# A two-layer hybrid trunk on one core: RWKV's loop in four array quarters, GLA sums before scores, value weights loaded earlier

## The chip, the core and the metric

One NeuronCore of a Trainium2 chip. The metric is the device time of one execution in microseconds, the median of three runs. A kernel here is a program of five engines with a queue each: TensorE (PE) for matrix products, VectorE (DVE), ScalarE (ACT), GpSimd (POOL) and SyncE (SP), which issues most loads.

## What is computed

A trunk of two layers on 512 tokens of width 1024, with a memory of 256 rows. Everything is float32. Layer 0 mixes with gated linear attention (GLA, 4 heads, keys of 64, values of 128) beside RWKV-7 (8 heads of 64), layer 1 with an RG-LRU beside an mLSTM. After each mixer come a cross attention to the memory and a gated FFN. Cut to what the change touches:

```python
# GLA, per chunk of 64: scores within the chunk, state across chunks
scores = where(causal, q_dec @ k_inv.T, 0);  o = scores @ v + q_dec @ S
S = S * state_decay + k_end.T @ v
# RWKV-7, per chunk
z = z_state @ S + z_local          # (I - A_ab)^-1 applied: a triangular solve
y = r_dec @ S + A_rb @ z + y_local
S = S * state_decay + z.T @ b_end + v.T @ k_end
# cross attention, both layers: k, v = split(rms_norm(mem) @ xattn_wkv[layer])
```

## The kernel before

Activations are held transposed, 128 channels by 512 tokens a tile. A dense product with a weight block is done as three passes in a reduced float32 form: the block (512 KB) is loaded by SP into a ring of three `raw` buffers, ScalarE rounds it to `wh`, VectorE takes the rest as `wl` (rings of two each), and TensorE adds wh·xh, wh·xl and wl·xh (`wload`, L238; `dense`, L258). All of these instructions stand under the helper lines L192 (VectorE tensor-tensor), L204 (ScalarE) and L207 (products), so groups are told apart by the names of their tiles. PSUM has eight banks: three called `mm` for dense products and five called `ax` for all the rest.

The order on each engine comes from a planner that goes by program order as priority and puts later instructions in where earlier ones would wait. `issue_after` keeps a few in a chosen place.

GLA (`gla`, L602) projects q, k, v, then per head pair `p` computes masked scores into `SC` (L700 to L708), then the chunk sums and the state scan `S` (L709 to L724), then the outputs.

RWKV (`rwkv`, L777) prepares its operands per head pair (L808 to L875): `stk` and `SV` for the two heads `e` of a pair, `BB` with the masked products. Then the triangular solve (L877 to L915): 32x32 blocks are inverted in 31 steps of two VectorE instructions (`tm`, `tu`), the result is transposed back (L896, L898), and two groups of 32x32 products join the two blocks of each 64. Then the loop over 8 chunks (L931 to L960): w = stk·SV, copied to `ws`; y's first half; z = BB·ws, copied to `SV`; the state sum `uu`; y's second half from BB and z, copied to `yt`. A 64x64 product of head `e` uses rows `R[e]` and columns `R[e]` of the array, that is, one of two diagonal quarters.

The memory's keys and values for both layers (`memory_k`, L528; `memory_v`, L548) come last in the program order of this part (`after`, L1306), and the planner lays them into the solve and the loop. Layer 0's keys are done from raw float32 weights without conversion, eight blocks in the `raw` ring; its values need `wh` and `wl`, 512 columns by two k-blocks a piece, two halves of four pieces.

## Time and profile before

| | us |
|---|---|
| median of 3 runs | 1544.91 (1544.68 to 1545.15) |
| profiled execution | 1545.02 |
| its span | 1543.2 |
| TensorE busy | 1518.2 (98%) |
| TensorE weight loads busy | 1235.4 (80%) |
| VectorE busy | 912.6 (59%) |
| ScalarE busy | 688.7 (45%) |

A product in float32 is run by TensorE as two passes, so 8 products are 16 records. "PE" is the products, "PEld" the weight loads that overlap them; since products are pipelined, the length of a group is better read from its weight loads. A merged row of the timeline gives the start, the busy time of the group, and in brackets how long the engine was idle before it and what ended that.

### The profile page before, as it was taken

To read this page: it belongs to the slowest core of one execution; us is meant where nothing else is said; L and a number is where in the kernel's file an instruction comes from. 1 tells how busy PE (TensorE), PEld (TensorE's weight loads), DVE (VectorE), ACT (ScalarE), POOL (GpSimd) and SP (SyncE) were. 2 spreads that over 40 slices of the span, in tenths; PEclk is the share of its full clock that TensorE was granted. 3 is DMA by queue.
4 is the path that set the end of the run, shared out by engine and by line. 5 is a ranking of instruction groups with operands and counts; after the bars stand their busy time and mean duration, and the time that the engine had idled before them with its cause. 6 is when DMAs were issued, how large, how long until landed. Compare 5 with 4: busy or idle time off the path is not lost.

```text
span 1543.2 us, 20154 instructions
## 1 busy us (share of the span) xinstructions
PE 1518.2 (98%) x8069; PEld 1235.4 (80%) x8069; DVE 912.6 (59%) x1341; ACT 688.7 (45%) x1105; POOL 25.5 (2%) x64
## 2 busy tenths in 40 slices
PE   9999998999999999999999999999999999999998
PEld 7977776778888888888888777788888888888887
DVE  7548679564645756555533377677457656565333
ACT  6466553364434633333322367556336333333322
POOL 2000000110000000000000000000000000000000
PEclk9999998999999999999999999999999999999999
DMA  5222235236421433333333421225114333333332
GB/s 179 69 75 84 67 103 158 90 116 227 137 62 48 124 96 96 96 96 100 89 100 97 121 63 56 75 75 175 45 55 123 96 96 96 96 96 91 101 99 79
DMA packets 49599, 152.19 MB, mean 99 GB/s; under 512 B 5489, under 2 KB 7953, under 8 KB 49505
## 3 DMA queue, kind: packets, MB, share of 16 engines
q1 hardware_dynamic: 45120, 142.28, 30.7%
q10 hardware_dynamic: 3248, 5.11, 0.9%
q0 software_dynamic: 1136, 3.51, 0.7%
q8 instruction: 63, 1.03, 0.3%
q14 instruction: 32, 0.25, 0.0%
HBM read 144.59 MB, written 6.29 MB: 98 GB/s over the span
## 4 chain that ended last, share of the span: by engine, by line
PE 87%; DVE 7%; ACT 3%; issue 2%; DMA 1%; POOL 0%; SPq 0%; DVEq 0%; ACTq 0%
PE mm L207 76%; PE ax L207 10%; DVE wl L192 1%; ACT wh L204 1%; PE ax L462 1%; DMA raw<-in_w_kv 0%; DVE tm L192 0%; ACT e L204 0%; DVE tu L192 0%; ACT xs L204 0%; DVE au L887 0%; DVE xs L192 0%; DMA x<-in_xT 0%; ACT a L204 0%; DVE stk L201 0%
## 5 line engine op out<-in xcount | busy, mean ns | idle before, releaser
L207 PE MATMUL mm<-xs,wh 128*128 128x512 f32 (+1 forms) x3627 | 1105.6, 386 | 0.0
L207 PEld LDWEIGHTS mm<-xs,wh 128*128 128x128 f32 x3627 | 672.0, 188 | 144.6 <-issue 7.2
L207 PE MATMUL mm<-xs,wl 128*128 128x512 f32 (+1 forms) x1814 | 701.2, 387 | 0.0
L204 ACT ACTIVATE wh<-raw 128x1024 fp32r<-128x1024 f32 (+2 forms) x274 | 265.0, 967 | 536.2 <-PE mm L207 429.1
L192 DVE TENSOR_TENSOR wl<-raw,wh 128x1024 fp32r<-128x1024 f32 (+2 forms) x273 | 302.6, 1109 | 216.7 <-ACT wh L204 215.7
L207 PEld LDWEIGHTS mm<-xs,wl 128*128 128x128 f32 x1814 | 340.8, 188 | 71.0 <-issue 2.4
L192 DVE TENSOR_TENSOR h<-h,mm 128x512 f32<-128x512 f32 (+1 forms) x73 | 49.5, 678 | 80.2 <-PE mm L207 80.2
L192 DVE TENSOR_TENSOR upad<-mm,rstd 128x512 f32<-128x512 f32 (+1 forms) x52 | 35.9, 690 | 95.5 <-PE mm L207 95.3
L192 DVE TENSOR_TENSOR g<-mm,rstd 128x512 f32<-128x512 f32 (+1 forms) x44 | 30.4, 692 | 76.0 <-PE mm L207 75.9
L201 DVE SCALAR_TENSOR_TENSOR c<-upad,vec,c 128x512 f32<-128x512 f32 (+1 forms) x88 | 65.9, 749 | 3.3 <-ACT c L204 1.8
L207 PE MATMUL mm<-wh,xs 128*128 128x256 f32 (+1 forms) x256 | 67.6, 354 | 0.0
L204 ACT ACTIVATE c<-c 128x512 f32<-128x512 f32 (+1 forms) x44 | 27.8, 632 | 87.1 <-DVE c L201 87.1
L207 PEld LDWEIGHTS mm<-wh,xs 128*128 128x128 f32 x256 | 45.1, 196 | 6.4 <-ACT kt L204 0.8
L207 PE MATMUL mm<-wl,xs 128*128 128x256 f32 (+1 forms) x128 | 45.1, 353 | 2.9 <-DVE wl L192 2.9
L204 ACT ACTIVATE xs<-g 128x512 fp32r<-128x512 f32 (+1 forms) x44 | 27.9, 633 | 26.6 <-DVE g L192 26.6
L192 DVE TENSOR_TENSOR xs<-ax,xs 128x512 fp32r<-128x512 f32 (+1 forms) x36 | 24.0, 686 | 20.8 <-ACT xs L204 20.8
L204 ACT ACTIVATE c<-upad,vec 128x512 f32<-128x512 f32 (+1 forms) x44 | 35.3, 803 | 1.5 <-DVE upad L192 1.5
L192 DVE TENSOR_TENSOR g<-c,g 128x512 f32<-128x512 f32 (+1 forms) x44 | 30.4, 692 | 5.8 <-ACT c L204 1.4
L192 DVE TENSOR_TENSOR nacc<-nacc,nsq 128x512 f32<-128x512 f32 x45 | 32.8, 729 | 0.7 <-ACT nsq L204 0.6
L201 DVE SCALAR_TENSOR_TENSOR xs<-h,vec,xs 128x512 fp32r<-128x512 f32 x40 | 29.9, 749 | 3.5 <-ACT xs L204 3.4
L204 ACT ACTIVATE xs<-h,vec 128x512 fp32r<-128x512 f32 x40 | 28.8, 719 | 6.6 <-DVE h L192 6.6
L192 DVE TENSOR_TENSOR xs<-g,xs 128x512 fp32r<-128x512 f32 (+1 forms) x44 | 30.1, 685 | 2.5 <-ACT xs L204 2.5
(354 smaller groups left out, 1194.0 us busy)
## 6 DMA issues: line engine op xcount, KB each, us to landing
raw<-in_w_up SPq DMA_DIRECT2D x86, 512.0 KB, 3.5
raw<-in_w_dn SPq DMA_DIRECT2D x32, 512.0 KB, 3.5
raw<-in_w_kk SPq DMA_DIRECT2D x16, 512.0 KB, 3.6
raw<-in_w_kv SPq DMA_DIRECT2D x16, 512.0 KB, 4.1
raw<-in_w_q SPq DMA_DIRECT2D x16, 512.0 KB, 3.7
raw<-in_w_o SPq DMA_DIRECT2D x32, 256.0 KB, 2.7
raw<-in_w_cd SPq DMA_DIRECT2D x16, 512.0 KB, 3.6
raw<-in_w_rw SPq DMA_DIRECT2D x14, 512.0 KB, 3.8
```

The source lines that it names most:

```text
L192: (eng or self.nc.vector).tensor_tensor(out=out, in0=a, in1=b, op=op)
L201: return self.nc.vector.scalar_tensor_tensor(out=out, in0=a, scalar=s, in1=b, op0=op0, op1=op1)
L204: return self.nc.scalar.activation(out=out, in_=a, func=f, **kw)
L207: self.last_mm = self.nc.tensor.matmul(out, lhsT=l, rhs=r, start=start, stop=stop)
L462: nc.tensor.transpose(pT[m][:, t * P:(t + 1) * P], es[t][:, m * P:(m + 1) * P], K.ident)
```

## The change

Four edits. `memory_k` of layer 0 calls a function ahead of its fifth block that issues the load and the conversion of the first two value pieces; `memory_v` uses them. In GLA, each head pair's chunk sums and state scan come ahead of its scores and masks. At the end of the solve one transposition of all 128 partitions into a new tile `TT` replaces four of 32 partitions into `BB`; four copies (two on each of VectorE and ScalarE) bring it to `BB`, placed behind the first product group, and the second group reads `TT`. In the loop, head pairs 2 and 3 write the other column half, so that z and y's second half use all four quarters; z and y have two banks each (z's second lies in w's bank), and their evictions are split accordingly; y becomes one tile.

```diff
--- before.py
+++ after.py
@@ -525,11 +525,13 @@
     return X
 
 
-def memory_k(K, l, X, stage):
+def memory_k(K, l, X, stage, midway=None):
 
     nc = K.nc
     kd = K.dram.tile([P, 2048], F32, name=f"kd{l}")
     for j in range(0, KD, 2):
+        if midway and j == 4:
+            midway()
         st = stage.tile([P, T], F32, name="kvs")
         for i in range(2):
             if type(X[0]) is tuple:
@@ -545,14 +547,18 @@
     return kd
 
 
-def memory_v(K, l, X, stage):
+def v_weights(K, l, half, c):
+    return K.wload(K.I[f"w_kv{l}"][:, half, 2 * c:2 * c + 2], 2, 512)
+
+
+def memory_v(K, l, X, stage, early=()):
 
     nc = K.nc
     vd = K.dram.tile([P, 2048], F32, name=f"vd{l}")
     for half in range(2):
         ps = [K.mm.tile([P, T], F32, name="mm") for _ in range(2)]
         for c in range(4):
-            wh, wl = K.wload(K.I[f"w_kv{l}"][:, half, 2 * c:2 * c + 2], 2, 512)
+            wh, wl = early[c] if half == 0 and c < len(early) else v_weights(K, l, half, c)
             for m in range(2):
                 ms = slice(m * P, (m + 1) * P)
                 for k in range(2):
@@ -697,15 +703,6 @@
                         K.mmul(o, xh[:, ts], wl[:, k], False, c == 1 and k == 3 and t % 2 == 1)
             for t in range(4):
                 K.act(v[:, t, half * 256:(half + 1) * 256], ps[t // 2][:, t % 2], AF.Copy, scale=rt[:, t:t + 1])
-        for p in range(2):
-            ps = [K.ax.tile([P, 4, P], F32, name="ax") for _ in range(2)]
-            for t in range(4):
-                ts = slice(t * P, (t + 1) * P)
-                for e in range(2):
-                    r = slice(64 * e, 64 * e + 64)
-                    K.mmul(ps[e][:, t], ki[p][r, ts], qd[p][r, ts])
-            for e in range(2):
-                nc.vector.copy_predicated(out=SC[2 * p + e], mask=gm.to_broadcast([P, 4, P]), data=ps[e])
         S = gp.tile([P, 2, 7, P], F32, name="S")
         for p in range(2):
             us = [K.ax.tile([P, 4, P], F32, name="ax") for _ in range(2)]
@@ -722,6 +719,15 @@
                     K.act(S[:, p, 0], u, AF.Copy)
                 else:
                     K.stt(S[:, p, c], S[:, p, c - 1], sd[p][:, c, 63:64], u, ALU.mult, ALU.add)
+            ps = [K.ax.tile([P, 4, P], F32, name="ax") for _ in range(2)]
+            for t in range(4):
+                ts = slice(t * P, (t + 1) * P)
+                for e in range(2):
+                    r = slice(64 * e, 64 * e + 64)
+                    K.mmul(ps[e][:, t], ki[p][r, ts], qd[p][r, ts])
+            for e in range(2):
+                nc.vector.copy_predicated(out=SC[2 * p + e], mask=gm.to_broadcast([P, 4, P]), data=ps[e])
+
         def outputs(p):
 
             os = [K.ax.tile([P, T], F32, name="ax") for _ in range(2)]
@@ -894,8 +900,8 @@
                 K.add(Tt[:, s + 1:, 0:s + 1], Tt[:, s + 1:, 0:s + 1], tv)
             TN = A
             nc.vector.transpose(out=TN.rearrange("p u c -> p c u"), in_=Tt.rearrange("p l c -> p c l"))
-            for q in (1, 3, 0, 2):
-                nc.vector.transpose(out=units[Q[q], :, H[q % 2]].rearrange("p u l -> p l u"), in_=Tt[Q[q]])
+            TT = sp.tile([P, 32, 32], F32, name="tt")
+            nc.vector.transpose(out=TT.rearrange("p u l -> p l u"), in_=Tt)
             VV = sp.tile([P, 32, 32], F32, name="vv")
             for b in range(2):
                 ps = K.ax.tile([P, 16, 32], F32, name="ax")
@@ -905,12 +911,17 @@
                         K.mmul(ps[Q[2 * e + 1], u], units[Q[2 * e], 16 * b + u, 32:64], TN[Q[2 * e], 16 * b + u])
                 for e in range(2):
                     K.act(VV[Q[2 * e + 1], us], ps[Q[2 * e + 1]], AF.Copy)
+            for q in range(4):
+                if q % 2:
+                    K.act(units[Q[q], :, H[1]], TT[Q[q]], AF.Copy)
+                else:
+                    nc.vector.tensor_copy(out=units[Q[q], :, H[0]], in_=TT[Q[q]])
             for b in range(2):
                 ps = K.ax.tile([P, 16, 32], F32, name="ax")
                 us = slice(16 * b, 16 * b + 16)
                 for u in range(16):
                     for e in range(2):
-                        K.mmul(ps[Q[2 * e], u], VV[Q[2 * e + 1], 16 * b + u], units[Q[2 * e + 1], 16 * b + u, 32:64])
+                        K.mmul(ps[Q[2 * e], u], VV[Q[2 * e + 1], 16 * b + u], TT[Q[2 * e + 1], 16 * b + u])
                 for e in range(2):
                     K.act(units[Q[2 * e], us, 32:64], ps[Q[2 * e]], AF.Copy)
         with ExitStack() as es:
@@ -919,7 +930,9 @@
             nc.vector.memset(S, 0.0)
             for e in range(2):
                 nc.vector.memset(SV[e][R[e], 0], 0.0)
-            yt = [st.tile([P, T], F32, name=f"y{p}", bufs=1) for p in range(4)]
+            yt = st.tile([P, 4, T], F32, name="y", bufs=1)
+
+            O = [(p, e, R[e if p < 2 else 1 - e]) for i in range(2) for p in (i, 2 + i) for e in range(2)]
 
             def group(products):
 
@@ -929,21 +942,21 @@
                         f()
 
             for c in range(8):
-                w = K.ax.tile([P, 4, 64], F32, name="ax")
-                yp = K.ax.tile([P, 4, 64], F32, name="ax")
+                w = K.ax.tile([P, 8, 64], F32, name="ax")
+                yp = [K.ax.tile([P, 2, 64], F32, name="ax") for _ in range(2)]
                 group([lambda e=e, p=p: K.mmul(w[R[e], p], stk[e][:, p, c, 0:64], SV[e][:, c, p])
                        for p in range(4) for e in (1, 0)])
                 ws = st.tile([P, 4, 64], F32, name="ws")
-                nc.vector.tensor_copy(out=ws, in_=w)
-                for p in range(4):
-                    for e in range(2):
-                        K.mmul(yp[R[e], p], SV[e][:, c, p], stk[e][:, p, c, 64:128], p == 0, False)
-                z = K.ax.tile([P, 4, 64], F32, name="ax")
-                for p in range(4):
-                    for e in range(2):
-                        K.mmul(z[R[e], p], BB[R[e], p, c, 0:64], ws[R[e], p])
-                nc.vector.tensor_copy(out=SV[0][R[0], c], in_=z[R[0]])
-                K.act(SV[1][R[1], c], z[R[1]], AF.Copy)
+                nc.vector.tensor_copy(out=ws, in_=w[:, 0:4])
+                for p, e, o in O:
+                    K.mmul(yp[p // 2][o, p % 2], SV[e][:, c, p], stk[e][:, p, c, 64:128], p % 2 == 0, False)
+
+                z = (K.ax.tile([P, 2, 64], F32, name="ax"), w[:, 4:6])
+                for p, e, o in O:
+                    K.mmul(z[p // 2][o, p % 2], BB[R[e], p, c, 0:64], ws[R[e], p])
+                for s, o in ((slice(0, 2), 0), (slice(2, 4), 1)):
+                    nc.vector.tensor_copy(out=SV[0][R[0], c, s], in_=z[o][R[o]])
+                    K.act(SV[1][R[1], c, s], z[o][R[1 - o]], AF.Copy)
                 if c < 7:
                     uu = K.ax.tile([P, 4, 64], F32, name="ax")
                     group([lambda e=e, p=p: K.mmul(uu[R[e], p], BKT[:, p, c, R[e]], SV[e][:, c, p])
@@ -954,14 +967,16 @@
                     for e in range(2):
                         K.mul(SV[e][R[e], c + 1], t[R[e]], sb[R[e]].to_broadcast([64, 4, 64]))
                     K.mul(S, t, sb.to_broadcast([P, 4, 64]), nc.gpsimd)
-                group([lambda e=e, p=p: K.mmul(yp[R[e], p], SV[e][R[e], c, p], BB[R[e], p, c, 64:128], False, p == 3)
-                       for p in range(4) for e in (1, 0)])
-                for p in range(4):
-                    K.act(yt[p][:, c * 64:c * 64 + 64], yp[:, p], AF.Copy)
+                group([lambda e=e, p=p, o=o: K.mmul(yp[p // 2][o, p % 2], SV[e][R[e], c, p], BB[R[e], p, c, 64:128],
+                                                           False, p % 2 == 1) for p, e, o in O])
+                cs = slice(c * 64, c * 64 + 64)
+                K.act(yt[:, 0:2, cs], yp[0], AF.Copy)
+                for e in range(2):
+                    K.act(yt[R[e], 2:4, cs], yp[1][R[1 - e]], AF.Copy)
             g2 = K.qr.tile([P, T], F32, name="xs")
             nc.gpsimd.dma_start(out=g2, in_=K.I["w_g2"])
             for p in range(4):
-                y = yt[p]
+                y = yt[:, p]
                 ps = K.ax.tile([P, T], F32, name="ax")
                 K.mmul(ps, K.bo64m, y)
                 K.tt(y, y, ps, ALU.subtract)
@@ -1304,11 +1319,13 @@
                 M[:] = next(M[0])
 
         def after(stage):
-            kv.append([memory_k(K, 0, [t[:, s] for t in M for s in (slice(0, 256), slice(256, 512))], stage)])
+            early = []
+            kv.append([memory_k(K, 0, [t[:, s] for t in M for s in (slice(0, 256), slice(256, 512))], stage,
+                                lambda: early.extend(v_weights(K, 0, 0, c) for c in range(2)))])
             for h in range(4):
                 Y[h] = K.split(K.pr[0], Y[h])
             ms = memory_split(K, M)
-            kv[0].append(memory_v(K, 0, ms, stage))
+            kv[0].append(memory_v(K, 0, ms, stage, early))
             kv.append([memory_k(K, 1, ms, stage), memory_v(K, 1, ms, stage)])
 
         rwkv(K, X, Y, during, after)
```

## Rows read from the trace of the kernel before

**Rows 1.** Page, part 1: busy us, share of the span, instructions.
```profile
PE 1518.2 (98%) x8069; PEld 1235.4 (80%) x8069; DVE 912.6 (59%) x1341; ACT 688.7 (45%) x1105; POOL 25.5 (2%) x64
```
**Rows 2.** Stretches: length, then each engine's busy time, granted clock, DMA.
```profile
241.00:244.00 3.00, 0.62 (x3) 0.22 (x2) 2.90 (x7) 1.33 (x2) 0.00 (x0) 1.00 0.23 87
244.30:247.70 3.40, 3.40 (x9) 2.65 (x9) 3.29 (x7) 0.00 (x0) 0.00 (x0) 0.50 0.81 261
247.80:256.80 9.00, 9.00 (x41) 7.43 (x40) 8.49 (x22) 4.41 (x6) 0.00 (x0) 1.00 0.68 207
257.00:263.20 6.20, 2.92 (x131) 2.37 (x129) 6.11 (x4) 1.90 (x3) 0.00 (x0) 0.85 0.48 136
261.40:275.00 13.60, 12.13 (x194) 9.46 (x195) 8.46 (x8) 4.96 (x8) 0.00 (x0) 0.50 0.13 41
```
**Rows 3.** Waits of PE, whole span: us in total, times, longest.
```profile
PE mm L207 <- DVE wl L192: 2.9, 2, 2.4
PE ax L207 <- issue: 2.5, 2, 1.9
PE ax L207 <- DVE au L896: 1.4, 1, 1.4
...
PE ax L207 <- DVE sc L708: 0.6, 1, 0.6
PE ax L207 <- DVE S L201: 0.6, 1, 0.6
```
**Rows 4.** Page, part 6: loads, KB each, median us from issue to landing.
```profile
raw<-in_w_kk SPq DMA_DIRECT2D x16, 512.0 KB, 3.6
raw<-in_w_kv SPq DMA_DIRECT2D x16, 512.0 KB, 4.1
```
**Rows 5.** Timeline, key blocks: start, us, engine, line, operation, tiles, count.
```profile
218.75 22.18 PE L207 MATMUL mm<-xs,raw 128*128 128x256 f32 x102
...
234.06 22.33 SPq L248 DMA_DIRECT2D raw<-in_w_kv  x8
```
**Rows 6.** Timeline, RWKV's preparation, weight loads of the 64x64 products.
```profile
213.03 0.85 PEld L207 LDWEIGHTS ax<-stk,bk 64*64 64x64 f32 x16 [0.53 <-DVE bk L192]
...
214.73 0.88 PEld L207 LDWEIGHTS ax<-stk,bk 64*64 64x64 f32 x16 [0.38 <-issue]
...
216.37 0.86 PEld L207 LDWEIGHTS ax<-stk,bk 64*64 64x64 f32 x32 [0.17 <-issue]
```
**Rows 7.** Timeline, end of the solve: transposes, 32x32 products, next wl.
```profile
256.65 2.12 DVE L896 STREAM_TRANSPOSE au<-tu 128x1024 f32<-128x1024 f32 x1
...
258.80 7.73 DVE L898 STREAM_TRANSPOSE bb<-tu 32x1024 f32<-32x1024 f32 x4
258.88 2.00 PEld L207 LDWEIGHTS ax<-au,bb 32*32 32x32 f32 x120 [1.80 <-issue]
...
265.77 3.48 PEld L207 LDWEIGHTS ax<-bb,vv 32*32 32x32 f32 x126 [0.65 <-issue]
266.56 1.23 DVE L192 TENSOR_TENSOR wl<-raw,wh 128x1024 fp32r<-128x1024 f32 x1
```
**Rows 8.** Timeline, one chunk of the loop: z, its evictions, a conversion between.
```profile
305.86 0.54 PEld L207 LDWEIGHTS ax<-ws,bb 64*64 64x64 f32 x16
...
306.59 0.42 DVE L945 COPY sv<-ax 64x256 f32<-64x256 f32 x1 [0.98 <-PE ax L207]
...
307.01 1.06 ACT L204 ACTIVATE wh<-raw 128x1024 fp32r<-128x1024 f32 x1 [3.21 <-PE mm L207]
...
308.10 0.38 ACT L204 ACTIVATE sv<-ax 64x256 f32<-64x256 f32 x1
```
**Rows 9.** Timeline, GLA: masks of the scores, first and later state steps.
```profile
64.32 2.54 DVE L708 COPY_PREDICATED sc<-gmask,ax 128x512 f32<-128x512 uint8 x4
...
66.07 0.28 ACT L204 ACTIVATE S<-ax 128x128 f32<-128x128 f32 x1 [2.20 <-PE ax L207]
...
66.77 4.23 DVE L201 SCALAR_TENSOR_TENSOR S<-S,eg,ax 128x128 f32<-128x128 f32 x12
```

## The prediction, made before the change was run

> **What bounds the kernel now.** I read the busy shares first: TensorE 98% of the span, its weight loads 80%, VectorE 59%, ScalarE 45% [rows 1]. TensorE sets the time, so an edit is worth what it takes off TensorE's own work, its idle time, or the time it runs at the lower clock. The profiled execution took 1545.02 us (span 1543.2, and 1.8 around it), 0.1 above the median of the three runs, 1544.91. Sums below start from 1545.02.
>
> The second view was a table of stretches around RWKV's triangular solve [rows 2]. Three places lose time. From 241 to 244 PE is busy 0.62 of 3.00 us. From 257 to 263.2 it is busy 2.92 of 6.20. And twice the granted clock is 0.50, the lower of its two levels (1.2 of 2.4 GHz): from 244.3 to 247.7, right after the first gap, and from 261.4 to 275.0, begun in the second one. Third, PE's waits say who ended the idle time [rows 3]: the low half of converted weights (wl) 2.9 us, nothing that the profile shows ("issue") 2.5, VectorE's 32x32 block transpose 1.4, and in the GLA stage two waits of 0.6 each. These are what the change can reach; the rest of the span is dense products that it doesn't touch.
>
> **Part 1, early value weights.** Before, the loads of layer 0's value weights follow all eight key loads on SP and start at 234.06 [rows 5], since three raw buffers feed them; VectorE, in the 62 small steps of the solve, delivers the first wl only at 243.7, and PE idles 2.4 us [rows 2, 3]. The 3.4 us at half clock that follow did work that takes 1.7 at full clock. So up to 2.4 + 1.7 = 4.1 us can go.
>
> What it adds: two loads are moved ahead of key blocks 4 to 7 in the same ring of three. A key block is 16 passes of 22.18/102 = 0.217 us, so 3.48 us [rows 5]. The keys end at 240.9; four blocks back, block 3 ends at 227.0. Before, block 4's load went out when block 1 was done (220.0). After, that buffer goes to the first value piece and block 2's (223.5) to the second, and block 4 has to wait for block 3's own buffer: out at 227.0, landing 3.6 us later [rows 4], at 230.6. For 3.6 us PE has no key block. What can cover it is the first value piece itself: out at 220.0, landed after 4.1 us [rows 4], wh 1.06 [rows 8], then wl 1.22 behind the transposes on VectorE, about 227.9. Its 12 products take 12 x 9.00/41 = 2.6 us [rows 2]. That leaves about 0.9 us uncovered. While the value sums hold two of the three "mm" banks, key blocks 5 to 7 share one and wait for its eviction, some 0.7 us each (an estimate: twice a ScalarE copy of 0.38, [rows 8], for the copy and the way there and back); the second piece's 12 products lie in those holes, so I cost them at nothing (2.1 us if they don't). One or two wl conversions more come before the end of the solve, 1.22 us of VectorE each, but each also gives PE 2.6 us of products while the solve runs late: nothing. Part 1: 4.1 - 0.9 = 3.2 us gained. Bounds: 5.5 (nothing uncovered and the 1.4 us transpose wait filled too), and a loss of 3.3 (3.6 idle, 1.7 of clock after it, 2.1 of evictions, against 4.1).
>
> **Part 2, end of the solve.** Before, VectorE runs one 128-partition transpose (2.12) and then four 32-partition ones (7.73), and the next wl comes at 266.56 [rows 7]. After, there is one more 128-partition transpose and two copies of 32x1024, with two such copies on ScalarE. A copy of this size isn't in the trace; between 0.42 (256 elements, [rows 8]) and 1.23 (a 128x1024 subtraction, [rows 7]) I take the upper, by its element count. So 2.12 + 2.46 = 4.6 instead of 7.7: VectorE, and with it the next wl, comes 3.1 us earlier. The second product group no longer waits for the copies at all, since it reads the transposed tile directly. ScalarE's copies (1.06 each by the conversion of 1024 columns, [rows 8]) lie where ScalarE waits for PE. What remains is the 1.9 us of "issue" inside the first product group, which no edit here removes. What goes back to PE is a part of the 13.6 us at 0.50: 120 passes took 2.00 us at full clock and 126 took 3.48 at the lower [rows 7], so the 12.1 busy us are worth some 6 at most. The 32x32 products that precede the drop are unchanged, so I expect the drop to come again and to end sooner: 2.0 us gained, a third of that. Bounds: 7.5 (all of it and the 1.4 us wait), and a loss of 1.2 (one wl put behind the copies).
>
> **Part 3, the loop in four quarters.** Per chunk two groups change, z and the second half of y: 8 products, 16 passes each. Now they use two diagonal quarters and take 0.54 us, 34 ns a pass [rows 8]. The trace has the same step elsewhere: in the preparation, 64x64 products of 128 columns run 16 passes in 0.85 and 16 in 0.88 when only one diagonal is in use, and 32 in 0.86 when all four quarters are [rows 6]: 53 against 27 ns a pass, twice the speed. For 64 columns no row has four quarters. The slow bound is those 27 ns (0.43 a group), the fast one the 17 ns a pass that 32x32 products reach [rows 7] (0.27). I take the middle, 0.35: 0.19 saved x 16 groups = 3.0 us.
>
> The Trainium skill (TensorEngine Tiling (Array Packing), "Instruction Overhead") says that each matmul carries about 60 cycles, so that tiling a dimension already short brings little. By it a pass would not go under 25 ns at 2.4 GHz, an estimate from that page, and a group would take 0.40. The 17 ns of [rows 7] contradict so high a floor here. By the page the part would give 2.2 us instead of 3.0.
>
> It also adds instructions: z is evicted in four pieces instead of two. One VectorE copy of 0.42 [rows 8] becomes two of about 0.35 (a 128x128 step of the GLA scan, [rows 9]), one ScalarE copy of 0.38 becomes two of 0.28 [rows 8, 9]; y's four copies become three. The chain from z to the state grows by 0.3 us a chunk. In that stretch PE runs memory products as filler (from 306.5 to 308.5 in the chunk shown, while ScalarE converts a weight ahead of its copy, [rows 8]), so I charge only 0.05 x 8 = 0.4. If filler ran out, it would be 8 x 0.3 = 2.4. The first half of y and the sums w and u contract over 128 and gain nothing. All five "ax" banks are now in use in a chunk instead of four, but the two banks a new chunk needs are evicted before its first product. Part 3: 2.6 us gained, bounds 4.3 and a loss of 2.4.
>
> **Part 4, GLA.** VectorE masks four score tiles (2.54) and only then scans the states (4.23) [rows 9]; PE waits 0.6 for a bank behind the masks and 0.6 for a bank behind the scan [rows 3]. With state sums first, head pair 0's outputs can start after 2.1 of scan and 1.3 of masks, one pair of masks (1.27) sooner. But VectorE's total is the same, and the last state sum of pair 1 now needs the fifth bank's successor, which comes free only as pair 0's scan ends. I take 0.7 of the 1.2 us; bounds 1.5 and a loss of 1.0.
>
> **Sum:** 3.2 + 2.0 + 2.6 + 0.7 = 8.5, so 1536.5, and by the median 1536.4 us.
>
> **Rivals.** *The clock and the quarters give little.* The half-clock stretch stays whole, the quarters run at 27 ns (16 x 0.11 - 0.4 = 1.4), GLA nothing, part 1 as forecast: 4.6 gained, 1540.4. For it: the small products around 261 are the same; against: VectorE is free 3 us earlier. *The gap only moves.* The 2.4 us and the 1.7 of clock go, but 3.6 come back at 227 because the program's order leaves the key blocks first: 0.5, with 1.4 from the quarters: 1543.1. For it: the value sums are later in the program than the keys; against: PE already takes later work when earlier work waits, the memory products in the loop among them. *Slower.* The starved ring at 227 drops the clock as the gap at 257 did: 3.6 idle, and 13.6 us at half clock behind it, 6.8, and 2.1 of evictions, so 12.5, against 4.1 + 2.0 + 2.6 + 0.7 = 9.4: 3.1 slower, 1548.1. It decides when the price at 227 exceeds 9.4; against it, the wait of 2.4 us at 241 cost only 3.4 us at half clock. *Upper ends.* 5.0 + 5.0 + 4.0 + 1.0 = 15: 1530.
>
> **How the numbers follow.** Forecast (1533 to 1539) 0.42, little gain 0.20, the gap moves 0.15, slower 0.10, upper ends 0.13. About 0.2%, 3.1 us, is what a measurement can tell from no change. The forecast, the upper ends and little gain are faster: 0.75. The gap that moves (1.9 us) is no change: 0.15; slower 0.10. The range of 1529 to 1544 leaves out the slower case and the far tails.
>
> **What would show it.** Part 1: no wait for wl near 241, value loads on SP at 220 and 223.5, clock 1.00 at 244 to 248; wrong, if PE idles over 2 us near 227 to 231. Part 2: the second group of 32x32 products starts within 4 us of the first, and the stretch at 0.50 is under 11 us. Part 3: z and second y groups of 0.27 to 0.43 us in place of 0.54. Part 4: the two waits of 0.6 gone. The forecast fails if the half clock lasts longer than before, or if the memory products run dry before the loop ends.

## The result, and the profile after

The changed kernel takes 1554.55 us (median of 4 runs, 1552.43 to 1554.90) against 1544.80 for the kernel before on the same chip: a ratio of 1.0067, interval 1.0054 to 1.0080. It is 10 us slower; 1536.4 was forecast, and the time lies outside the range of 1529 to 1544. The profiled execution took 1554.81 (span 1553.0). Medians here and below leave out four slow executions, of 1609 to 4746 us, of two kernels below.

First the busy shares and PE's waits, to be held against [rows 1, 3].

```profile
PE 1523.1 (98%) x8069; PEld 1235.3 (80%) x8069; DVE 909.4 (59%) x1348; ACT 695.0 (45%) x1107; POOL 25.6 (2%) x64
```

Waits of PE over the span of the changed kernel (us in total, times, longest):

```profile
PE mm L207 <- DMA raw<-in_w_kk: 5.8, 1, 5.8
PE ax L207 <- issue: 2.8, 2, 2.1
PE mm L207 <- DVE wl L192: 1.5, 2, 1.0
PE ax L207 <- DVE au L902: 1.4, 1, 1.4
...
PE ax L207 <- DVE sc L729: 1.1, 1, 1.1
```

The 2.4 us wait for wl is gone, as forecast. In its place stands one wait of 5.8 us for a key block. The two GLA waits of 0.6 have become one of 1.1. The "issue" is still there. The 1.5 us for wl, and 0.7 for wh besides, now lie behind the loop, where the kernel before has 0.5.

Stretches of the changed kernel (length, busy time of PE, PEld, DVE, ACT, POOL, granted clock, DMA):

```profile
227.90:230.70 2.80, 0.53 (x3) 0.13 (x1) 2.77 (x7) 1.50 (x3) 0.00 (x0) 1.00 0.05 20
230.70:237.50 6.80, 3.23 (x8) 2.63 (x9) 6.25 (x19) 0.00 (x0) 0.00 (x0) 0.50 0.85 272
249.60:258.70 9.10, 9.10 (x42) 7.52 (x41) 8.45 (x24) 3.27 (x4) 0.00 (x0) 1.00 0.52 144
...
260.70:266.30 5.60, 5.60 (x260) 4.86 (x260) 3.93 (x4) 4.26 (x6) 0.00 (x0) 1.00 0.38 117
268.30:281.90 13.60, 13.20 (x115) 9.26 (x117) 4.02 (x8) 4.14 (x10) 0.70 (x1) 0.50 0.14 45
```

Around the solve and the loop there are again two stretches at 0.50, the lower level of 1.2 GHz, and again each begins in or right behind idle time of PE. The first now follows the key wait and lasts 6.8 us instead of 3.4 [rows 2]. The second is as long as before (13.6), but it has moved from the 32x32 products into the loop.

The timeline, read at a few places of both kernels, says how the 10 us come about (starts of products; an end is the start of the product that follows):

| until | before, us | after, us | later by |
|---|---|---|---|
| end of GLA's products | 77.8 | 79.0 | 1.3 |
| end of the key blocks | 240.6 | 249.6 | 9.0 |
| first 32x32 product | 258.9 | 260.7 | 1.8 |
| first product of the loop | 269.3 | 266.3 | -3.1 |
| end of the loop | 322.4 | 324.0 | 1.6 |
| end of the memory products | 366.6 | 376.7 | 10.1 |
| last product | 1535.4 | 1545.2 | 9.8 |

The loss of 9 us at the keys seems to be healed at the first 32x32 product, and comes back behind the loop. The solve is VectorE's chain, which a late PE hardly touches, so the 32x32 products start at almost the same time. What PE didn't do by then is value products: they are the filler, they were pushed behind the loop, and the stretch from the loop's end to the end of the memory products grew from 44.2 to 52.7 us.

SP's loads, VectorE's and PE's operations at the key blocks of the changed kernel (start, us, engine, line, operation, count):

```profile
180.11 32.73 SPq L541 DMA_DIRECT2D raw<-in_w_kk  x4
221.55 3.79 SPq L248 DMA_DIRECT2D raw<-in_w_kv  x2
229.93 10.00 SPq L541 DMA_DIRECT2D raw<-in_w_kk  x4
```

```profile
224.01 3.92 DVE L893 STREAM_TRANSPOSE au<-bb 32x1024 f32<-32x1024 f32 x2
227.97 0.69 DVE L192 TENSOR_TENSOR xs<-xs 128x512 fp32r<-128x512 f32 x1
...
228.69 1.21 DVE L192 TENSOR_TENSOR wl<-raw,wh 128x1024 fp32r<-128x1024 f32 x1
```

```profile
234.27 15.66 PE L207 MATMUL mm<-xs,raw 128*128 128x256 f32 x64 [5.84 <-DMA raw<-in_w_kk]
249.58 0.81 PE L207 MATMUL mm<-wh,xs 128*128 128x512 f32 x2
```

Key block 4's load goes out at 229.93. PE was through with block 3 at 228.4; what the load waited for is, by these times, the first early piece's conversion, whose last reader on VectorE, the wl of 228.69, ends at 229.90. SP's own waits agree:

```profile
SPq L541 <- DVE tu L192: 7.0, 2, 4.3
```

So two of the four later key loads wait for VectorE (the row names the last event that VectorE had recorded), which stands in the middle of the solve. The load between these two, whose buffer was free, stands behind the first in SP's order. And the value products come at 249.58, after the last key block: none of them filled the hole.

### The profile page after: what moved, and what is told of

Its sections match the earlier page's. It is cut to its first block, busy times and chain, and to the rows that moved or that the text cites. A ratio compares the mean times of both kernels' runs of the same rounds, so it can differ in the third digit from the quotient of the medians.

```text
span 1553.0 us, 20156 instructions
## 1 busy us (share of the span) xinstructions
PE 1523.1 (98%) x8069; PEld 1235.3 (80%) x8069; DVE 909.4 (59%) x1348; ACT 695.0 (45%) x1107; POOL 25.6 (2%) x64
## 4 chain that ended last, share of the span: by engine, by line
PE 88%; DVE 6%; ACT 3%; issue 1%; DMA 1%; SPq 0%; POOL 0%; DVEq 0%; ACTq 0%
PE mm L207 77%; PE ax L207 10%; DVE wl L192 1%; PE ax L462 1%; ACT wh L204 1%; DMA raw<-in_w_kv 1%; ACT e L204 0%; ACT xs L204 0%; DMA x<-in_xT 0%; DVE au L893 0%; DVE xs L192 0%; ACT a L204 0%; DMA lgw<-in_w_lg 0%; DMA raw<-in_w_kk 0%; DVE stk L201 0%
## 5 line engine op out<-in xcount | busy, mean ns | idle before, releaser
L207 PE MATMUL mm<-xs,raw 128*128 128x256 f32 x128 | 30.1, 395 | 5.8 <-DMA raw<-in_w_kk 5.8
L207 PEld LDWEIGHTS mm<-xs,raw 128*128 128x128 f32 x128 | 25.2, 199 | 10.4 <-issue 6.9
```

The source lines that it names most:

```text
L207: self.last_mm = self.nc.tensor.matmul(out, lhsT=l, rhs=r, start=start, stop=stop)
```

## The experiments

Times are medians, each beside the kernel before, measured with it (1544.3, 1544.4, 1544.5 and 1544.7 in four sets). One execution of each kernel was profiled, and it need not be one near the median.

### The parts one at a time

**Early value weights alone** (of the change only `memory_k`, `memory_v` and `after`).

```diff
+        if midway and j == 4:
+            midway()
...
+                                lambda: early.extend(v_weights(K, 0, 0, c) for c in range(2)))])
```

> The kernel before with the early value pieces alone. Theory A: one wait of PE of 5 to 6 us for the load of key block 4 and a stretch at half clock behind it; slower than before, 1549 to 1551. Rival B: within 1.5 us of before.

Measured: 1547.30, ratio 1.0025 (1.0016 to 1.0033), between the two forecasts. The key blocks end at 249.8, after a wait for a key block of

```profile
PE mm L207 <- DMA raw<-in_w_kk: 6.1, 1, 6.1
```

The part alone makes the hole, and alone it is slower by about 3 us. The first of its later key loads goes out at 228.86, again right behind the end of a wl on VectorE (228.84).

**All but the early value weights.**

```diff
-                                lambda: early.extend(v_weights(K, 0, 0, c) for c in range(2)))])
...
-            kv[0].append(memory_v(K, 0, ms, stage, early))
+            kv[0].append(memory_v(K, 0, ms, stage))
```

> The whole change without the two early value pieces. Theory A (the ring of three raw buffers starves the key blocks, and that is most of the 10 us): no wait of PE for a key block's load, the keys end within 1.5 us of where they did before (240.8), the clock stays whole around 230 to 237, and the time falls by about 6 from the changed kernel's 1554.5, to 1547 to 1550; the wait for wl near 241 is back. Rival B (the loop's split evictions scatter the small products between the memory products, and that is most of it; the early pieces break even): 1552 or more.

Measured: 1550.27, ratio 1.0039 (1.0028 to 1.0051), a little over theory A's range and under the rival's. No wait for a key block is left, and the clock is whole from 230 to 237; the profiled execution has 20.5 us at half clock from 260 on. So more than half of the loss has other causes.

**The loop in four quarters alone** (of the change only what begins at `yt`).

```diff
+            O = [(p, e, R[e if p < 2 else 1 - e]) for i in range(2) for p in (i, 2 + i) for e in range(2)]
...
+                for s, o in ((slice(0, 2), 0), (slice(2, 4), 1)):
+                    nc.vector.tensor_copy(out=SV[0][R[0], c, s], in_=z[o][R[o]])
+                    K.act(SV[1][R[1], c, s], z[o][R[1 - o]], AF.Copy)
```

> The kernel before with the loop's four quarters alone. Theory A: z groups of 0.39 us instead of 0.61, and 2 to 3 us faster than before, 1542. Rival B: z is as short, but y's second half and the state sum run in pieces between memory products, 8 to 11 changes of product shape a chunk instead of 6, and what a chunk costs beside the memory products stays at 3.8 us or rises to 4.2: 1545 to 1548.

Measured: 1547.78, ratio 1.0027 (1.0016 to 1.0038), rival B's time. The part that was to give 2.6 us costs 3.5. The profiled execution is the fastest of the six, 1545.97. A chunk of it on PE (start, us, operation, count):

```profile
299.10 0.46 PE L207 MATMUL ax<-ws,bb 64*64 64x64 f32 x16
...
300.05 0.33 PE L207 MATMUL ax<-bb,sv 64*64 64x64 f32 x2
300.30 0.38 PE L207 MATMUL mm<-xs,wl 128*128 128x256 f32 x1
300.61 0.45 PE L207 MATMUL ax<-sv,bkt 128*64 128x64 f32 x8
301.00 0.44 PE L207 MATMUL ax<-bb,sv 64*64 64x64 f32 x8
...
302.27 0.45 PE L207 MATMUL ax<-sv,bkt 128*64 128x64 f32 x8
302.66 0.44 PE L207 MATMUL ax<-bb,sv 64*64 64x64 f32 x6
```

The z group is as quick as forecast: from its start to the next product 0.40 us, 0.62 before. But the u sums (`sv,bkt`) and the second y group (`bb,sv`) have come apart. z is now evicted in two halves, a product is ready with its half, and the fixed order of PE puts memory products between. Two passes at 300.05 take 0.25 us until the next product starts, where their share of a whole group would be 0.05. Chunks with a split order have 8 or 10 changes of shape between large and small products instead of 6. Those with 10 take 4.2 us beside their memory products; the kernel before takes 3.5 to 3.8.

**The end of the solve alone** (of the change only `TT`, its copies and the second product group).

```diff
-            for q in (1, 3, 0, 2):
-                nc.vector.transpose(out=units[Q[q], :, H[q % 2]].rearrange("p u l -> p l u"), in_=Tt[Q[q]])
+            TT = sp.tile([P, 32, 32], F32, name="tt")
+            nc.vector.transpose(out=TT.rearrange("p u l -> p l u"), in_=Tt)
```

> The kernel before with the end of the solve alone. If the 4.5 us less between the first 32x32 product and the first product of the loop are a gain: 1540 to 1541. If the stretch at half clock only moves on into the loop and takes them back (it is as long in the changed kernel, 13.7 us, and 7 us later): 1543 to 1545.

Measured: 1545.93, ratio 1.0006 (0.9996 to 1.0016): nothing gained, and a little over both forecasts. Its timeline, against [rows 7]:

```profile
258.88 1.89 DVE L898 STREAM_TRANSPOSE tt<-tu 128x1024 f32<-128x1024 f32 x1
...
260.64 1.19 DVE L192 TENSOR_TENSOR wl<-raw,wh 128x1024 fp32r<-128x1024 f32 x1
261.76 1.35 DVE L912 COPY bb<-tt 32x1024 f32<-32x1024 f32 x2
263.07 0.42 PE L207 MATMUL ax<-au,bb 32*32 32x32 f32 x8 [1.51 <-issue]
...
264.58 0.18 PEld L207 LDWEIGHTS ax<-tt,vv 32*32 32x32 f32 x2 [0.65 <-ACT vv L204]
...
265.97 3.62 PE L207 MATMUL ax<-tt,vv 32*32 32x32 f32 x126
...
269.52 1.12 PE L207 MATMUL ax<-sv,stk 128*64 128x64 f32 x16
```

VectorE is through at 263.1 instead of 266.5, and the next wl comes 5.9 us earlier. But the second product group starts when it did (265.97 against 265.77) and takes as long, at half clock; the loop's first product is at 269.52 against 269.32. The group hadn't waited for the transposes: in both executions it waited 0.65 us for ScalarE's vv, behind the "issue" (264.37 in the kernel before).

**GLA alone** (the score products and their masks behind each head pair's state sums).

```diff
         S = gp.tile([P, 2, 7, P], F32, name="S")
         for p in range(2):
...
+            for e in range(2):
+                nc.vector.copy_predicated(out=SC[2 * p + e], mask=gm.to_broadcast([P, 4, P]), data=ps[e])
```

> The kernel before with the GLA part alone (state sums ahead of scores). Theory, from the changed kernel's trace, where the two waits of 0.6 became one of 1.1 and one of 1.6 of the weight load, and the stage ended 1.3 us later: 0.5 to 1.5 us slower, 1545 to 1546, the last GLA product at about 78.8 instead of 77.6. Rival (that lateness came from another execution's noise): 0.7 us faster, as forecast, 1543.6.

Measured: 1545.27, ratio 1.0008 (0.9999 to 1.0017). The interval holds no change. As in the changed kernel, one wait of 1.1 for VectorE's masks stands where two of 0.6 were: the masks now come last, and the outputs wait for them. Whether this costs the 0.9 us that the median shows stays open, since the stage ends anywhere between 77.6 and 78.7 in kernels without this edit.

The profiled execution matters for another reason. It is the fastest of ten, 1541.72, and its end of the solve is that of the kernel before, yet there the clock held until 270 and no "issue" stood:

```profile
262.00:268.00 6.00, 5.30 (x166) 3.94 (x165) 5.92 (x4) 4.31 (x8) 0.00 (x0) 1.00 0.03 5
```

From the first 32x32 product to the loop 6.0 us passed instead of 10.4. So one trace per kernel can't say by itself that an edit made the clock fall or hold.

By medians the parts alone add up to 3.0 + 3.5 + 1.6 + 0.9 = 9.0, and the change measures 9.8. Each interval is 2.6 us wide or more, so whether the parts act on one another isn't shown.

### What in the early loads costs

**One early piece instead of two.**

```diff
-                                lambda: early.extend(v_weights(K, 0, 0, c) for c in range(2)))])
+                                lambda: early.extend(v_weights(K, 0, 0, c) for c in range(1)))])
```

> The kernel before with one early value piece instead of two. Theory (two pieces in the ring of three raw buffers leave one for the keys, so key block 4's load goes out 3 to 10 us late): with one piece two buffers stay for the keys, no wait of PE for a key block exceeds 1 us, the keys end at 241 to 243 instead of 250, and the time is within 1.5 us of the kernel before or up to 2 under it, 1542.5 to 1546. Rival (what costs is the conversions that VectorE does in the middle of the solve, or the value products not being placed among the keys at all): 1547 again, with the keys on time and the loss behind them.

Measured: 1544.27, ratio 1.0000 (0.9991 to 1.0008); the keys end at 243.5.

```profile
220.68 0.33 SPq L248 DMA_DIRECT2D raw<-in_w_kv  x1
224.13 7.81 SPq L541 DMA_DIRECT2D raw<-in_w_kk  x4
```

```profile
PE mm L207 <- DMA raw<-in_w_kk: 2.0, 2, 1.6
PE mm L207 <- DVE wl L192: 1.2, 1, 1.2
```

The time is the theory's. The waits are not: I expected none over 1 us and one of 1.6 remained. One piece exchanges the wait of 2.4 us at 241 for 0.3 at 228, 1.6 at 233 and 1.2 for a wl later.

**Two pieces, apart.**

```diff
-        if midway and j == 4:
+        if midway and j in (2, 6):
-                                lambda: early.extend(v_weights(K, 0, 0, c) for c in range(2)))])
+                                lambda: early.append(v_weights(K, 0, 0, len(early))))])
```

> The kernel before with two early value pieces, but apart: one ahead of key block 2 and one ahead of key block 6, instead of both ahead of block 4. Theory (what starves the keys is that two of three buffers hold value pieces at once until VectorE has converted them): no wait for a key block over 2 us, keys end at 242 to 245, 1543 to 1545.5, like the run with one piece. Rival (the number of early pieces counts, not their distance): keys end at 248 or later, 1547.

Measured: 1543.89, ratio 0.9998 (0.9990 to 1.0007). The keys end at 245.4, the longest wait is

```profile
PE mm L207 <- DMA raw<-in_w_kk: 2.5, 2, 2.2
```

Both a little beyond what the theory allowed, and far from the rival's 248 and 1547. So it is two pieces in the ring at once that starve it, not their number. A ring of four or a ring of the value pieces' own wasn't tried.

### What in the loop costs

**The loop part with its groups whole.** The u sums and the second y products begin with a product of the half that is evicted last:

```diff
+            O2 = [(p, e, R[e if p < 2 else 1 - e]) for i in (1, 0) for p in (2 + i, i) for e in (1, 0)]
...
-                           for p in range(4) for e in (1, 0)])
+                           for p in (3, 2, 1, 0) for e in (1, 0)])
...
-                                                           False, p % 2 == 1) for p, e, o in O])
+                                                           False, p % 2 == 0) for p, e, o in O2])
```

> The kernel before with the loop part alone, whose u sums and second y products are put in another order: the group begins with a product of the half of z that is evicted last, so that the whole group becomes ready at once. Theory (the quarters' gain is eaten by groups that come apart, each piece costing a change of tile shape): the second y group runs in one piece of about 0.32 us in every chunk, the changes of shape per chunk fall from 8 to 11 back to 6 to 8, a chunk beside memory products takes 3.3 to 3.7 us, and the time is 1 to 3 us under the kernel before, 1541 to 1543. Rival (the loss has to do with the chain through VectorE and ScalarE or with PE's clock, not with pieces): 1546 to 1549 as with the loop part as it is.

Measured: 1544.79, ratio 1.0002 (0.9994 to 1.0011), 3 us under the loop part as it was.

```profile
306.42 0.69 PE L207 MATMUL ax<-sv,bkt 128*64 128x64 f32 x16
307.03 0.46 PE L207 MATMUL ax<-bb,sv 64*64 64x64 f32 x16
...
309.00 0.42 PE L207 MATMUL ax<-sv,stk 128*64 128x64 f32 x7 [0.47 <-DVE sv L192]
```

Six changes of shape in every chunk: the scattering is shown. But 1541 to 1543 was expected. The loop ends at 319.3 instead of 322.4, and the memory products at 366.2 instead of 366.6. Behind the loop PE now waits for converted weights (the kernel before has 0.5 there):

```profile
PE mm L207 <- DVE wl L192: 1.0, 2, 0.5
PE mm L207 <- ACT wh L204: 0.5, 1, 0.5
```

One us is given back by these waits, since the filler's own weights come no earlier. More is given back in the loop itself. All chunks but the first now begin with a wait of 0.3 to 0.5 us for VectorE's state:

```profile
PE ax L207 <- DVE sv L192: 2.8, 7, 0.5
```

The kernel before has 0.3 of it in two waits, the loop part as it was 0.6. A chunk of the kernel before shows why:

```profile
308.53 0.69 PE L207 MATMUL ax<-sv,bkt 128*64 128x64 f32 x16
...
311.11 0.69 PE L207 MATMUL ax<-sv,stk 128*64 128x64 f32 x16
```

From the u sums to the next chunk's first product 2.58 us pass there, and 2.58 in the mended loop (306.42 to 309.00), since VectorE's state is ready only 0.15 us before that product in both (310.96 and 308.85). The second y group lies in this time; when it is quicker, PE waits for the rest. So of the 16 x 0.22 = 3.5 us that the quicker groups save, about 2.5 come back as waits for the state and 1.0 as waits behind the loop.

**Both mends in all four parts.**

> All four parts, with one early value piece instead of two and the loop's u and second y groups in the order of the last evicted half. Theory (the starved ring and the scattered groups are the loss): keys on time, y2 in one piece, the quarters' saving kept, 1541 to 1545, so 9 us or more under the changed kernel. Rival (the parts' losses add up through something else, such as the half clock that now lies in the loop): 1549 or more.

Measured: 1546.26, ratio 1.0011 (1.0002 to 1.0021): some 8 of the 10 us are the ring and the scattered groups. The time lies between the two forecasts; the 1.9 left are about the end of the solve and GLA alone (1.6 and 0.9, neither clear of noise).

### Why the end of the solve gives nothing

**Two added products ahead of the 32x32 products**, in the kernel before. Their result isn't used; they run while VectorE transposes.

```diff
             TN = A
+            dm = K.ax.tile([P, T], F32, name="ax")
+            for _ in range(2):
+                K.mmul(dm, K.ident, flat(Tt)[:, T:])
```

> The kernel before with two added 128x128 by 128x512 products whose result nobody reads, over the second half of the finished solve, so that they run while VectorE makes the 128-partition transpose for which PE waits 1.4 us. Theory (the end of the solve costs what it costs because PE's thin stretch drops the clock, and the drop is worth 5 to 8 us of work): the stretch at 0.50 that begins near 261 is gone or under 7 us, the first 32x32 product comes no more than 0.5 us later than 258.9, and the time is 2 to 6 us under the kernel before, 1538 to 1542. Rival (the 32x32 products and the 1.9 us of issue drop the clock whatever runs ahead of them): stretch as long as before, time 1544 to 1546.

Measured: 1544.82, ratio 1.0004 (0.9995 to 1.0013). The clock still fell, for 10.2 us: the rival's number.

**Two more, one after each half of the first 32x32 group.**

```diff
                 for e in range(2):
                     K.act(VV[Q[2 * e + 1], us], ps[Q[2 * e + 1]], AF.Copy)
+                K.mmul(dm, K.ident, flat(A)[:, 0:T])
```

> As the run with two added products, with two more between the halves of the 32x32 products, over the transposed tile; these lie on PE's path, about 1 us each. Theory: the clock holds through the end of the solve, first loop product at 266 to 268 instead of 269.3, 1539 to 1543. Rival (the drop comes whatever the products are, and each added product costs its time): 1546 to 1548.

Measured: 1542.67, ratio 0.9994 (0.9985 to 1.0002), all eleven runs between 1542.0 and 1543.5. The clock holds:

```profile
258.90:266.00 7.10, 6.89 (x261) 4.95 (x260) 6.99 (x5) 3.53 (x6) 0.00 (x0) 1.00 0.23 84
266.00:275.00 9.00, 7.64 (x133) 5.78 (x129) 5.10 (x9) 3.18 (x8) 0.70 (x1) 1.00 0.21 62
```

From the first 32x32 product to the loop 6.8 us pass instead of 10.4, with two useless products of 1.1 each on the path. Then VectorE is what is late:

```profile
259.16 7.76 DVE L901 STREAM_TRANSPOSE bb<-tu 32x1024 f32<-32x1024 f32 x4
...
266.94 1.23 DVE L192 TENSOR_TENSOR wl<-raw,wh 128x1024 fp32r<-128x1024 f32 x1
...
268.36 0.36 DVE L941 COPY ws<-ax 128x256 f32<-128x256 f32 x1
268.87 0.68 PE L207 MATMUL ax<-ws,bb 64*64 64x64 f32 x16 [1.27 <-DVE ws L941]
```

**The end of the solve with the two products.**

> The end-of-solve part with the two added products. Theory (that part's gain of 3 us on VectorE reaches the path only when the clock holds, since at half clock PE's 32x32 products end later than VectorE does either way): faster than the run with the added products alone by 0.5 to 2 us, first ws copy of the loop under 268.5 instead of 270.5, 1537 to 1541. Rival (the part brings nothing at either clock): the same time as the run with added products alone, within 0.5 us, or later.

Measured: 1544.86, ratio 1.0002 (0.9992 to 1.0012). By the median a miss. But its runs spread from 1539.7 to 1547.7, and in the profiled one, 1539.70, the clock happened to hold:

```profile
265.22 0.69 PE L207 MATMUL ax<-sv,stk 128*64 128x64 f32 x16
...
265.95 0.42 DVE L945 COPY ws<-ax 128x256 f32<-128x256 f32 x1 [0.21 <-PE ax L207]
```

ws comes 2.4 us earlier than in the execution above. There the edit is worth what it takes off VectorE. All executions taken together point the same way: at a mean granted clock of 0.997 or 0.998 kernels with this edit and at most two added products took 1538.4 to 1541.4 us (six executions), those with the old end of the solve and no added product 1541.6 and 1541.7 (two). With so few, a gain where the clock holds is likely but not shown.

**The end of the solve with the four products.**

> The end-of-solve part with four added products, two ahead of the 32x32 products and two between their halves, as in the run with four over the kernel before (1542.67, granted clock 0.50 nowhere in this stretch). Theory (with the clock held, the earlier VectorE is the path: the loop's first ws copy came at 265.95 in the one execution of the end-of-solve part in which the clock held, 268.36 without the part): 1.5 to 3 us faster than 1542.7, so 1539.5 to 1541.5. Rival (the part brings nothing at either clock, or drops the clock again): 1542.5 or more.

Measured: 1543.91, ratio 0.9999 (0.9991 to 1.0008): the rival's number, for a third reason. The clock holds, but PE's waits from 256 to 272 are now

```profile
PE ax L207 <- issue: 1.9, 2, 1.0
PE ax L207 <- DVE tu L192: 0.7, 1, 0.7
```

and ws comes at 269.22. With the four products alone no "issue" stands in this stretch; in the changed kernel one of 2.1 stands at the loop's first products, and with GLA alone none is seen. Its place goes with the program: at the 120th pass of the 32x32 products in the kernel before, in the loop part alone and in the end of the solve alone, and at the same two places to within a pass, 127 passes apart, in the three kernels with this end of the solve and four added products. What PE then waits for no view shows, and it stays open. Nor does the clock hang on it alone: with early weights alone, with both mends and without the early weights none of it stands in this stretch, and the clock fell all the same, for 10.2, 10.2 and 20.5 us; here it stands, and the clock held.

**Combinations:** one early piece, the end of the solve, the mended loop and two products;

> One early value piece, the end of the solve, the loop in the order of the last evicted half, no GLA part, and the two added products. Theory (all that cost is mended and the clock holds): 1536 to 1541, under the kernel before by 3 us or more. Rival (what holds the clock in one place drops it in the next, in the loop's first chunks): 1544 to 1547.

Measured: 1544.90, ratio 1.0001 (0.9993 to 1.0010), again with 10.2 us at half clock: the rival's number. The end of the solve, the mended loop and four products, without early weights and GLA:

> End of solve, loop in the order of the last evicted half, and the four added products; no early value weights, no GLA part. Theory (with the clock held the loop's saving of 0.15 us a chunk, 1.2 in all, comes on top of that of the end of the solve): 1538.5 to 1541, 3.5 us or more under the kernel before, and up to 1 us under the run with the end of solve and four products. Rival (the loop's saving is given back as waits for converted weights behind the loop, 1.0 us there already): the same as that run.

Measured: **1541.13, ratio 0.9981 (0.9972 to 0.9990)**, a little over the forecast and faster than both kernels: 3.5 us under the kernel before, 13 under the changed one. It is 2.8 faster than the same without the loop part, so there the quarters do pay; behind the loop PE waits 0.5 us for weights, as in the kernel before. Why it is more than the 1.2 of the theory isn't shown. Its loop, like the mended one above, waits for the state's chain,

```profile
PE ax L207 <- DVE sv L192: 2.6, 7, 0.5
```

one wait of 0.3 to 0.5 in every chunk but the first. The same with one early piece:

> As the run with end of solve, loop in the order of the last evicted half and four added products, with one early value piece besides. Theory (one piece exchanges 2.4 us of waiting near 232 for 2.2 us near 241): within 0.7 us of that run. Rival (the extra wait in the middle of the solve drops the clock in some executions): 1 to 3 us slower than it.

Measured: 1541.78, ratio 0.9982 (0.9974 to 0.9991): the theory's time.

## Why the prediction was wrong

**Part 1 (3.2 gained; measured about 3.0 lost).** The step that failed: "What can cover it is the first value piece itself". It was costed on when data would be there, and PE's order is fixed when the program is built: the value products stand behind the key blocks (249.58), ready or not. The wait was 5.8 us where 0.9 was allowed. Second, I let block 4 wait for block 3's buffer (227.0). By the times it was given the first value piece's, which VectorE frees; the piece's load went out at 221.55 instead of 220.0, its wl had to wait for the very transposes that the text named (to 227.93) and a conversion of xs behind them, and it ended at 229.90 instead of "about 227.9". Third, the clock: 6.8 us at 0.50 behind the hole, which cost some 3.4, where the forecast had none. And the 1.7 us that were to come back at 244 were less than counted. The wait of 2.4 for wl is in all eleven traces of kernels with the value loads in their old place, but the clock fell behind it in three of them only; where it held, PE waited 0.6 to 0.7 us more for the next wl. The *Slower* rival had the place and the mechanism, an idle PE and a clock that falls behind it. Its sizes were not right: 3.6 idle where 5.8 were measured, and a cost of 6.8 for the clock where 3.4 were; that its 1548.1, meant for the whole change, is near the 1547.3 of early weights alone is luck. The ground against it, that "PE already takes later work when earlier work waits", mixed up two things: the filler of the loop was put there by the order beforehand, not by PE.

**Part 2 (2.0 gained; measured between 0.6 gained and 2.5 lost, by the interval).** VectorE's saving was there, and larger than forecast: 7.73 us became 1.89 + 1.35 = 3.2, where 4.6 was forecast. The failed step is that it shortens the half-clock stretch. It didn't: the profiled execution of this part alone was at 0.50 for 17.1 us from 260.6 on, and PE's second group waited for ScalarE's vv, not for VectorE. Where the clock held, the 2.4 us at ws appeared. In the full change the 32x32 products did run at 1.00 and within 5.6 us, and the test that I named (the second group within 4 us of the first) came true; but the other test, under 11 us at 0.50, did not: the drop of 13.6 came 7 us later, in the loop.

**Part 3 (2.6 gained; measured 3.5 lost).** The price of a group was right: weight loads of 0.33 for the forecast 0.35. To the start of the next product a group went from 0.62 to 0.40, 25 ns a pass. By the 60 cycles of the Trainium skill (TensorEngine Tiling (Array Packing), "Instruction Overhead") I had 0.40 for a group, an estimate from that page, and called that contradicted: start to start it is what the trace shows here, and only the weight loads alone (0.33) lie under it. The 32x32 products do go under it, start to start too: 128 passes in 2.14 us in the changed kernel, 17 ns each. What failed is the 0.05 a chunk for the evictions. They were costed by their duration on VectorE and ScalarE, and their price is the order: a group whose products become ready in two halves is no longer one group. With the order mended, what is left is the term that the prediction named and put aside, "If filler ran out, it would be 8 x 0.3 = 2.4": PE waits 2.8 us for the state, where the kernel before waits 0.3. The size is right, the reason is not: from the u sums on the chain takes the 2.58 us that it took before, and it is PE that comes to its end sooner.

**Part 4 (0.7 gained; measured 0.9 lost, not clear of noise).** The two waits of 0.6 were to go; one of 1.1 stayed, because the outputs now wait for the masks. The size is within what can't be told apart.

## What to carry to other kernels

Ask of an early load whose buffer it takes and which engine gives that back: a ring shared between a stream that TensorE frees and one that a busy VectorE frees runs at the pace of the second. Where the order is fixed beforehand, data that is there early covers nothing unless its consumer was also placed early. Splitting an eviction makes a group of small products ready in pieces; begin the group with a product of the last piece, so that it stays whole. A group that runs while a chain on another engine is awaited gives nothing when it gets quicker. And an engine freed 3 us earlier is worth nothing while something on the other engine, here the half clock and an unexplained "issue", ends later.

## What the runs showed of the hardware

How long the clock stays at 0.50 differs between executions of one kernel, and with it the time: the kernel with the end of the solve and two added products ran in 1539.7 to 1547.7 us, the fastest at a mean granted clock of 0.998, those over 1545 at 0.993 to 0.995. The drop at the end of the solve was costly: without it, 3.6 us less passed from the first 32x32 product to the loop, added products included, and 4.4 less in the one execution with none of them. In the four profiled executions with four of these the clock stayed at 1.00 from 258 until 268 at least; in one of them (the fastest kernel's) it fell for 3.4 us in the loop's first chunk. The mean granted clock of every execution agrees: of the kernel before, 126 of 127 had 0.993 to 0.996, and the 44 of the four kernels with four added products had 0.995 to 0.999. That the drop can be kept off in every execution isn't shown.

A change between large products and a short piece of small ones costs PE about 0.2 us each way: in the loop part alone two passes of a 64x64 product held it 0.25 us where their share of a whole group is 0.05, and the one pass of a memory product behind them 0.31 where such a pass takes 0.12 among its like. Sixteen 64x64 passes in a row took 0.39 to 0.40 in four quarters and 0.61 to 0.62 in two.
